# Moving three groups of work in a hybrid decoder block: where two gates are kept, how long prefetched operands rest, and which units take the seven-product steps

## The chip, the cores and the metric

The kernel runs on one core of a Trainium2 chip. The metric is the device time of one execution in microseconds (us); lower is better. Several runs of a kernel are taken and their median is compared.

## The reference, cut to what matters

The input `x` is 256 tokens by 4096 channels, float32. `w_in` is 4096 by 20480, the two matrices in `w_branch` are 2048 by 4096, `w_out` is 4096 by 4096; all are float32 and each is read once.

```python
h = rmsnorm(x, norm_w)
u_p, z_p, u_c, b_c, c_c, z_c, g_logit = split(h @ w_in)      # widths 6 x 2048, then 8192
y_pool = pool(u_p, pool_w, pool_scale) * silu(z_p)           # trailing means over 2, 4, 8, 16 tokens, a linear map per group
y_conv = b_c * conv3(c_c * u_c) * silu(z_c)                  # causal depthwise convolution of width 3
gates  = sigmoid(g_logit.reshape(256, 2, 4096) + gate_b)
merged = gates[:, 0] * (y_pool @ w_branch[0]) + gates[:, 1] * (y_conv @ w_branch[1])
out    = rmsnorm(x + merged @ w_out, final_norm_w)
```

## The kernel before, in words

**Units.** The work is a row of *units*, each giving 256 tokens by 1024 output channels. Their order: `cz0 cb0 cu0 cc0 cz1 cb1 cu1 cc1` (convolution branch: the silu gate z, then b, u, c), `pz0 pu0 pz1 pu1` (pooling branch), `g0_0 g1_0 g0_1 g1_1 g0_2 g1_2 g0_3 g1_3` (gate `g{branch}_{column}`), `b0_0 b1_0 b0_1 b1_1 ... b1_3` (the branch projections), `o0` to `o3` (the output projection). The list `units` fixes the order; everything is issued in program order on each engine.

**Steps.** A unit goes through its input channels in steps of 256; a step loads one 1 MB tile of weights into one of three buffers of `raw`. Every float32 operand is split into a rounded part ("high") and a remainder ("low"), and each product is made of three TensorE matmuls of 128x128 by 128x512. A unit's text has one letter a step. `P` is a plain step: eight products, 24 matmuls; the weights need four highs (ScalarE, `highs`) and four lows (VectorE, `lows`). `S` is a step in the Strassen-Winograd form: seven products, 21 matmuls; VectorE also makes the four sums of weight blocks in the tile `parts` (its Python name is `sums`) and splits them, and part of the results goes to the `shared` PSUM banks. `B` and `M` are the pooling steps, put into `pz1` and `g0_0` (text `HOST`). So a letter turned from P to S takes three matmuls from TensorE and gives VectorE more to do. Split weights lie in `ring`, 15 cells; `pump` prepares steps up to `AHEAD` = 4 ahead, and three past the last step of a branch unit, as far as cells and buffers are free. The first `x` units (all `c`, `p` and `g` units) have 16 steps, as have the `o` units; the branch units have 8.

**End of a unit.** The four `sums` PSUM banks are copied to the unit's destination by ScalarE (`evacuate`, into `E`, or `Y` where `dst=Y`), at the unit's end and in ScalarE's program order; the next unit's first matmuls reuse those banks. The `shared` banks go to `J` and are summed on VectorE. For a unit with `late` set, `J` is added to the destination by an accumulating DMA (`gather`, on GpSimd's queue) and the scale follows later; else VectorE adds it at once. What remains of the unit, its *epilogue* (`epi`), is a list of small tasks; one is taken from `queue` at every *tick*, that is every 6 matmuls, while the next unit multiplies.

**Gates.** A gate unit's epilogue adds the bias by DMA, waits some ticks, applies Sigmoid in `E` and stores `E` to `gates_d` in DRAM. Branch unit `b0_c` multiplies its result by gate 0, which has been brought back into `Y`, and `b1_c` multiplies by gate 1, brought back into `last_pair` (the view `spare()`). In `g1_3`'s epilogue gate `gates_d[0, 0]` is brought into `Y`. `Y` is not used by any gate unit after `g0_0`, in which the last pooling step leaves it.

**Fills.** The stationary operands sit in `arena`, whose place is shared: as the last `x` unit and later the branch units finish with their operands, those of the branch units (`y_ops`) and of `o0` (`m_ops`) are read from DRAM and split in their place. Each is a `Fill`: `fetch` moves 256 KB into a staging tile (`sa` or `sb`), and `advance` works on it at later ticks, not before `LANDING` = 8 ticks after the fetch: sums of blocks on VectorE (S operands only, four ticks then pass), then one rounding on ScalarE (`arena<-sa` in the traces), a tick later one subtraction on VectorE, after which the staging tile is free for the next fetch. `pop_fill` makes at most one advance and one fetch a tick. The fetches are issued on GpSimd's queue, in program order with the gate and bias moves.

```python
st = next((q for q in stages if not any(q is u for u in used)), None)
if st is not None:
    nxt.fetch(st)
```

**The end.** The last three steps of `o3` are taken apart by token half; after them come the last sums, the norm and the stores (`finish_half`, `finish`).

Lines in the profile: L1012 the matmuls, L57 every ScalarE activation (`act`), L60 VectorE's tensor-tensor operations (`tt`), L75 loads on SyncE's queue, L81 moves and L84 accumulating moves on GpSimd's queue.

Of the kernel before, what the change touches and what calls it, by code (L numbers as in the profile page):

```python
# [15 lines left out]
P = 128  # L16
# [15 lines left out]
TAIL = 3  # L32

SIX5 = "PPPPPSPSPSPSPSPS"
FIRST = (0, 1, 8, 2, 9, 3, 10, 11, 4, 12, 13, 5, 14, 6, 15, 7)
OPENED = 12
EIGHT3 = "PPPSPSPSSPSPSSPS"
NINE = "PSPSPSPSSPSPSSPS"
NINE_A = "PSPSSPSPSSPSPSPS"
HOST = "PPPBPPMMPSPSSPSSPSS"  # L40
TEN = "PSPSSPSSPSSPSSPS"
OUT3 = "PSPSPSPSSPSSSPPP"
B0 = "PPPPSPSP"
B1 = "PSPSPSPP"
B1_FIRST = "PPSPSPSP"
# [4 lines left out]
def hybrid_block(ctx: ExitStack, tc: tile.TileContext, x, xc, prm, rows_in, w_in, pool_w, w_branch, w_out, out):  # L50
# [32 lines left out]
    def gather(dst, src):  # L83
        return pin(nc.gpsimd.dma_start(dst, src, accum_op=ALU.add))  # L84
# [391 lines left out]
    def gap(n):  # L476
        return [None] * n
# [39 lines left out]
    def in_unit(name, col, epi, text, **kw):  # L517
        units.append(Unit(name, lambda i: w_in[col // NU, i], seq_x(text), x_ops, epi, scaled=True, **kw))
        units[-1].text = text
        return units[-1]  # L520
# [15 lines left out]
    def silu_y(late):  # L536
        def silu(t):
            act(Y[:, t], Y[:, t], AF.Silu, **(dict(scale=rin[:, t:t + 1]) if late else {}))
        return gap(18 if late else 3) + [lambda: silu(0), None, lambda: silu(1)]
# [5 lines left out]
    def conv_units(c, first):  # L545
        base = 2 * HALF + c * NU

        def b_epi(u):
            def product(t):
                stt(E[:, t], E[:, t], rin[:, t:t + 1], Y[:, t], ALU.mult, ALU.mult)  # L550
            return gap(18) + [lambda: product(0), None, lambda: product(1), None, lambda: move(g_d[c], E)]

        def c_epi(u):
            def inner(j):
                if j == 3:
                    for i in range(4):
                        act(chan(E)[:, 2 * i:2 * i + 2], bankview(i))

            def outer(j):
                act(chan(J)[:, 2 * j:2 * j + 2], bankview(j))  # L560

            def taps(j):
                v, y = chan(E)[:, 2 * j:2 * j + 2], chan(Y)
                for i in range(2):
                    b = 2 * j + i
                    kb = 8 * c + b
                    act(y[:, b], v[:, i], AF.Identity, scale=tap_col(2, kb), bias=bias_col(kb))
                for s in (1, 2):
                    for i in range(2):
                        b = 2 * j + i  # L570
                        kb = 8 * c + b
                        stt(y[:, b, s:], v[:, i, 0:T - s], tap_col(2 - s, kb), y[:, b, s:], ALU.mult, ALU.add)

            items = [lambda: move(Y, g_d[c])] + gap(6) + pairs(transposes(E, inner)) + gap(5) + pairs(transposes(Y, outer))
            for j, n in enumerate((1, 7, 8, 8)):
                items += gap(n) + [lambda j=j: taps(j)]
            return items + [None, lambda: mul(chan(E), chan(J), chan(Y)), lambda: put(y_d[1, c], chan(E))]

        u = in_unit(f"cz{c}", base + 3 * HALF, lambda u: silu_y(u.late) + (gap(4) + side_items(ND - 1) + side_items(ND - 2) if first else []),
                    FIRST if first else SIX5, dst=Y)  # L580
        u.late = not first
        in_unit(f"cb{c}", base + HALF, b_epi, TEN if c else NINE_A).late = True
        u = in_unit(f"cu{c}", base, lambda u: rescale(Y), NINE, dst=Y)
        u.late = True
        in_unit(f"cc{c}", base + 2 * HALF, c_epi, NINE_A).urgent = lambda: mul(E, E, Y)

    def pool_units(c):
        u = in_unit(f"pz{c}", HALF + c * NU, lambda u: silu_y(True) + gap(4) + band_items(c), HOST if c else SIX5, dst=Y)
        u.late = True
        in_unit(f"pu{c}", c * NU, lambda u: [], NINE).urgent = lambda: None  # L590

# [92 lines left out]
            queue.extend(gap(3) + transposes(Y, copy) + [lambda: put(y_d[0, c], chan(E))])  # L684

    def gate_unit(n, c):
        def epi(u):
            def bias(t):
                gather(E[:, t], gate_b[n, None, c * NU:(c + 1) * NU].to_broadcast([P, NU]))

            pause = gap(12)
            if (n, c) == (1, 3):
                pause = gap(5) + [lambda: move(Y, gates_d[0, 0])] + gap(6)
            items = (rescale(E) if u.late else gap(1)) + [lambda: bias(0), lambda: bias(1)] + pause + [
                lambda: act(E[:, 0], E[:, 0], AF.Sigmoid), None,
                lambda: act(E[:, 1], E[:, 1], AF.Sigmoid), lambda: move(gates_d[n, c], E)]
            return items
        text = HOST if (n, c) == (0, 0) else EIGHT3 if (n, c) == (1, 3) else TEN
        u = in_unit(f"g{n}_{c}", 6 * HALF + n * D + c * NU, epi, text)
        u.late = (n, c) != (1, 3)  # L700

    def spare():
        return last_pair["tile"].rearrange("p (a n) -> p a n", a=2)
# [1 line left out]
    def branch_unit(n, c):  # L705
        def epi(u):
            if n == 0:
                return gap(8) + [lambda: mul(Y, E, Y), None, lambda: move(spare(), gates_d[1, c])]
            turned = spare() if c < 3 else Y

            def gated():
                mul(E, E, spare())
                if c == 3:
                    last_pair["stack"].close()
                    open_last(F32R)
                    last_pair["again"] = True

            def copy(j):
                act(chan(turned)[:, 2 * j:2 * j + 2], bankview(j))

            def stored():
                put(m_d[c], chan(turned))
                merged[c] = now[0] + STORED
            return gap(2) + [gated, None, lambda: add(E, E, Y), None,
                lambda: c < 3 and move(Y, gates_d[0, c + 1])] + gap(3) + pairs(transposes(E, copy)) + [stored]

        text = (B1_LAST if c == 3 else B1 if c else B1_FIRST) if n else B0
        u = Unit(f"b{n}_{c}", lambda i: w_branch[n, c, i], seq_y(text), y_ops[n], epi)
        u.urgent, u.lead = (lambda: None), 3
        units.append(u)  # L730
# [65 lines left out]
    stages = [sa]  # L796
    fills = deque()
    now, quiet, hush = [0], [0], [0]
    LANDING, STORED, QUIET, HUSH = 8, 7, 5, 14

    def pop_fill(force=None):
        now[0] += 1
# [13 lines left out]
    conv_units(1, False)  # L816
    for c in range(2):
        pool_units(c)
    for c_ in range(4):
        for n_ in range(2):  # L820
            gate_unit(n_, c_)
    last_x = units[-1]
    for c in range(4):
        branch_unit(0, c)
# [259 lines left out]
    for u in units:  # L1084
        if u.name == "b0_0":
            last_pair["stack"].close()
            open_last(F32)
        if u is names["o1"]:
            assert not fills
            more.close()  # L1090
            open_side()

            j, items = ND - 1, list(queue)
            queue.clear()
            sides = (gap(HUSH) + [lambda: move(sa[:, 4:].rearrange("p o c -> p (o c)"),
                                                   m_d[j // 4][:, j % 4].rearrange("p k t -> p (k t)"))] + gap(8) + [
                lambda: sums_s(sa), None, None, lambda: act(side["tile"][:, 0], sa[:, 0:4]), None,
                lambda: sub(side["tile"][:, 1], sa[:, 0:4], side["tile"][:, 0].bitcast(F32))])
            items += gap(len(sides) - len(items))
            sides += gap(len(items) - len(sides))  # L1100
            queue.extend([lambda a=a, b=b: (a and a(), b and b()) for a, b in zip(items, sides)])
        if u is names["g1_0"]:
            bands_open.close()
        if u is last_x:
            side["stack"].close()
            more = ExitStack()
            ctx.enter_context(more)
            stages.append(more.enter_context(tc.tile_pool(name="more", bufs=1)).tile([P, 8, P], F32, name="sb"))
            queue_fills()
        if u is last:  # L1110
            break
        for st in u.steps:
            assert st.prepared, (u.name, st.kind)
            run_step(u, st)
            if u.text is TEN and st.kind == "S" and st.op in x_ops[:ND] and st is not u.steps[-1]:
                side_load(2 * ND - 3 - x_ops.index(st.op))
            state["now"] += 1
            if state["now"] == OPENED:
                opening.close()
                sums = ctx.enter_context(tc.tile_pool(name="parts", bufs=1)).tile([P, 4, NH], F32, name="parts")  # L1120
                open_side()
            pump()
            if u.before and st is u.steps[len(u.steps) * 3 // 4]:
                flush()
                u.before()
        flush()
        combine(u)
        queue.extend(u.epi(u))
        pump()
# [102 lines left out]
```

## Time and profile before

| what | value |
|---|---|
| median of 3 runs | 2368.66 us (2367.86 to 2369.8) |
| the profiled execution's own time | 2370.85 us |
| its span, first to last instruction | 2369.1 us |
| mean granted TensorE clock | 0.997 |
| matmuls and transposes | 10436 |
| VectorE busy | 2207.6 us (93% of the span) |
| ScalarE busy | 1538.3 us (65%) |
| moved by DMA | 570.48 MB, mean 241 GB/s |

The profiled execution's time is 1.75 us more than its span and 2.19 us above the median of the runs. An engine that is busy for nearly all the span can only give time back where it waits, so the page is read with the list of waits and with the busy time of single units. Starts in the traces are us from the first instruction; a group's idle time stands in brackets with what ended it.

### The profile page before, as it was taken

What the parts mean: (1) busy time and instruction counts of PE and PEld (TensorE: products, weight loads), DVE (VectorE), ACT (ScalarE), POOL (GpSimd) and SP (SyncE); (2) the same over time, 40 slices, a digit from 0 to 9 for tenths busy, and PEclk for the clock granted to TensorE, in tenths of its full rate; (3) what the DMA queues carried; (4) which work ended last, traced back from release to release, by engine and by line L of the source; (5) the groups of instructions that cost most, each with busy time, mean ns of one, the idle gap of its engine ahead of it and who ended that gap; (6) DMA issues with size and microseconds to landing.
All of it is one profiled execution on the core that took longest, in us unless ns stands there. A gap on an engine that the chain in (4) does not pass through costs nothing. (4 is left out here: it accounts for less than half of the span.)

```text
span 2369.1 us, 28319 instructions
## 1 busy us (share of the span) xinstructions
PE 2345.7 (99%) x10436; PEld 1941.2 (82%) x10436; DVE 2207.6 (93%) x2433; ACT 1538.3 (65%) x1829; POOL 132.2 (6%) x193
## 2 busy tenths in 40 slices
PE   9999999999999999999999999999999999999997
PEld 7888888888888888888888888888878888888886
DVE  8899989999979979979999999999988898899998
ACT  6666656666666656656677767776655656566665
POOL 0000000000001000000000000001100001000000
PEclk9999999999999999999999999999999999999999
DMA  9667755775756656646877788778866757667886
GB/s 348 234 234 241 227 198 213 243 242 218 233 211 215 229 175 226 227 177 228 269 249 262 244 270 257 254 252 275 286 225 237 265 208 253 244 212 262 269 260 258
DMA packets 94330, 570.48 MB, mean 241 GB/s; under 512 B 10288, under 2 KB 10544, under 8 KB 33264
## 3 DMA queue, kind: packets, MB, share of 16 engines
q1 hardware_dynamic: 69824, 485.39, 56.8%
q0 software_dynamic: 23792, 82.06, 13.3%
q8 instruction: 81, 1.33, 0.2%
q10 hardware_dynamic: 576, 1.24, 0.1%
q14 instruction: 57, 0.47, 0.1%
HBM read 523.56 MB, written 27.26 MB: 233 GB/s over the span
## 5 line engine op out<-in xcount | busy, mean ns | idle before, releaser
L1012 PE MATMUL sums<-ring,arena 128*128 128x512 f32 x7071 | 1655.2, 390 | 9.2 <-ACT E L57 6.5
L1012 PEld LDWEIGHTS sums<-ring,arena 128*128 128x128 f32 x7071 | 1326.9, 188 | 286.2 <-ACT E L57 7.9
L60 DVE TENSOR_TENSOR ring<-raw,ring 128x1024 fp32r<-128x1024 f32 (+2 forms) x889 | 965.2, 1105 | 96.3 <-ACT ring L57 95.5
L57 ACT ACTIVATE ring<-raw 128x1024 fp32r<-128x1024 f32 (+3 forms) x682 | 790.7, 1196 | 229.4 <-PE sums L1012 111.4
L57 ACT ACTIVATE ring<-parts 128x512 fp32r<-128x512 f32 (+1 forms) x670 | 500.2, 761 | 484.7 <-DVE parts L60 425.3
L1012 PE MATMUL shared<-ring,arena 128*128 128x512 f32 x2193 | 529.5, 389 | 0.0
L60 DVE TENSOR_TENSOR ring<-parts,ring 128x1024 fp32r<-128x1024 f32 (+1 forms) x464 | 515.2, 1152 | 4.6 <-ACT ring L57 4.5
L1012 PEld LDWEIGHTS shared<-ring,arena 128*128 128x128 f32 x2193 | 411.7, 188 | 85.4
L60 DVE TENSOR_TENSOR parts<-parts,raw 128x512 f32<-128x512 f32 x436 | 297.7, 683 | 0.0
L60 DVE TENSOR_TENSOR parts<-raw 128x1024 f32<-128x1024 f32 x218 | 265.2, 1217 | 12.2 <-DMA raw<-in_w_in_dram 5.5
L60 DVE TENSOR_TENSOR J<-J 128x512 f32<-128x512 f32 (+1 forms) x90 | 78.1, 868 | 9.2 <-ACT J L57 6.3
L1012 PE MATMUL sums<-ring,last_pair 128*128 128x512 f32 x306 | 76.3, 389 | 0.6 <-DVE ring L60 0.6
L57 ACT ACTIVATE J<-shared 128x512 f32<-128x512 f32 x128 | 69.2, 604 | 2.3 <-PE shared L1012 0.5
L1012 PEld LDWEIGHTS sums<-ring,last_pair 128*128 128x128 f32 x306 | 57.4, 188 | 12.9 <-DVE ring L60 1.1
L84 POOL DMA_DIRECT2D E<-J x24 | 29.2, 1456 | 463.3 <-DVE J L60 324.9
L1012 PE MATMUL shared<-ring,last_pair 128*128 128x512 f32 x216 | 52.2, 390 | 0.0
L1012 PE MATMUL shared<-ring,side 128*128 128x512 f32 x207 | 50.7, 389 | 0.0
L57 ACT ACTIVATE E<-sums 128x512 f32<-128x512 f32 x80 | 44.8, 594 | 4.8 <-PE sums L1012 2.3
L1012 PEld LDWEIGHTS shared<-ring,last_pair 128*128 128x128 f32 x216 | 40.5, 188 | 8.8 <-DVE ring L60 0.4
L1012 PEld LDWEIGHTS shared<-ring,side 128*128 128x128 f32 x207 | 38.9, 188 | 8.1
L57 ACT ACTIVATE E<-E 128x1024 f32<-128x1024 f32 x20 | 20.9, 1046 | 4.6 <-DMA E<-in_x_dram 4.6
L84 POOL DMA_DIRECT2D Y<-J x10 | 12.2, 1453 | 199.2 <-issue 126.4
(132 smaller groups left out, 637.2 us busy)
## 6 DMA issues: line engine op xcount, KB each, us to landing
raw<-in_w_in_dram SPq DMA_DIRECT2D x318, 1024.0 KB, 4.9
raw<-in_w_branch_dram SPq DMA_DIRECT2D x64, 1024.0 KB, 4.8
raw<-in_w_out_dram SPq DMA_DIRECT2D x64, 1024.0 KB, 4.9
E<-J POOLq DMA_DIRECT2D x24, 512.0 KB, 8.3
E<-in_rows_dram POOLq DMA_DIRECT2D x16, 512.0 KB, 8.9
gates_d<-E POOLq DMA_DIRECT2D x8, 1024.0 KB, 6.5
Y<-J POOLq DMA_DIRECT2D x10, 512.0 KB, 9.5
y_d<-E POOLq DMA_DIRECT2D x8, 512.0 KB, 7.8
```

The costliest lines, as they stand in the source:

```text
L57: return pin(nc.scalar.activation(dst, src, func, **kw))
L60: return pin(nc.vector.tensor_tensor(out=dst, in0=a, in1=b, op=op))
L84: return pin(nc.gpsimd.dma_start(dst, src, accum_op=ALU.add))
L1012: pin(nc.tensor.matmul(ps, lhs, rhs, start=n == 0, stop=n == u.total[b] - 1))
```

## The change

- **Gates.** The order of the gate units becomes `g0_0 g0_1 g1_1 g0_2 g1_2 g0_3 g1_3 g1_0`. `g0_0` has `Y` as its destination and its gate stays there; `g1_0`, now the last `x` unit and the one that isn't late, writes its Sigmoid from `E` into `spare()`. These two gates are neither stored nor brought back; the pause in the epilogue of the last gate unit has no move of `Y` any more.
- **Fills.** `LANDING` is 12 ticks and not 8, and there is a third staging tile, `sc`.
- **Texts.** `cz1` and `pz0` have seven S steps and not six (`SIX5` to `SEVEN5`; `o0` keeps `SIX5`), the last gate unit has seven and not eight (`EIGHT3` to `SEVEN3`), `o3` has seven and not eight (`OUT3`).

```diff
+SEVEN5 = "PPPPPSPSSPSPSSPS"
-EIGHT3 = "PPPSPSPSSPSPSSPS"
+SEVEN3 = "PPPSPSPSPSPSPSPS"
-OUT3 = "PSPSPSPSSPSSSPPP"
+OUT3 = "PSPSPSPSPSPSSPPP"
...
-                    FIRST if first else SIX5, dst=Y)
+                    FIRST if first else SEVEN5, dst=Y)
...
-        u = in_unit(f"pz{c}", ..., HOST if c else SIX5, dst=Y)
+        u = in_unit(f"pz{c}", ..., HOST if c else SEVEN5, dst=Y)
...
     def gate_unit(n, c):
+        first, final = (n, c) == (0, 0), (n, c) == (1, 0)
+
         def epi(u):
+            d = u.dst
+
             def bias(t):
-                gather(E[:, t], gate_b[n, None, c * NU:(c + 1) * NU].to_broadcast([P, NU]))
-
-            pause = gap(12)
-            if (n, c) == (1, 3):
-                pause = gap(5) + [lambda: move(Y, gates_d[0, 0])] + gap(6)
-            items = (rescale(E) if u.late else gap(1)) + [lambda: bias(0), lambda: bias(1)] + pause + [
-                lambda: act(E[:, 0], E[:, 0], AF.Sigmoid), None,
-                lambda: act(E[:, 1], E[:, 1], AF.Sigmoid), lambda: move(gates_d[n, c], E)]
-            return items
-        text = HOST if (n, c) == (0, 0) else EIGHT3 if (n, c) == (1, 3) else TEN
-        u = in_unit(f"g{n}_{c}", 6 * HALF + n * D + c * NU, epi, text)
-        u.late = (n, c) != (1, 3)
+                gather(d[:, t], gate_b[n, None, c * NU:(c + 1) * NU].to_broadcast([P, NU]))
+
+            def gate(t):
+                act((spare() if final else d)[:, t], d[:, t], AF.Sigmoid)
+
+            items = (rescale(d) if u.late else gap(1)) + [lambda: bias(0), lambda: bias(1)] + gap(12) + [
+                lambda: gate(0), None, lambda: gate(1)]
+            return items if first or final else items + [lambda: move(gates_d[n, c], E)]
+        text = HOST if first else SEVEN3 if final else TEN
+        u = in_unit(f"g{n}_{c}", 6 * HALF + n * D + c * NU, epi, text, dst=Y if first else E)
+        u.late = not final
...
-                return gap(8) + [lambda: mul(Y, E, Y), None, lambda: move(spare(), gates_d[1, c])]
+                return gap(8) + [lambda: mul(Y, E, Y), None, lambda: c and move(spare(), gates_d[1, c])]
...
-    LANDING, STORED, QUIET, HUSH = 8, 7, 5, 14
+    LANDING, STORED, QUIET, HUSH = 12, 7, 5, 14
...
-    for c_ in range(4):
-        for n_ in range(2):
-            gate_unit(n_, c_)
+    gate_unit(0, 0)
+    for c in range(1, 4):
+        for n in range(2):
+            gate_unit(n, c)
+    gate_unit(1, 0)
...
-        if u is names["g1_0"]:
+        if u is names["g0_1"]:
             bands_open.close()
...
-            stages.append(more.enter_context(tc.tile_pool(name="more", bufs=1)).tile([P, 8, P], F32, name="sb"))
+            pool = more.enter_context(tc.tile_pool(name="more", bufs=1))
+            stages.extend(pool.tile([P, 8, P], F32, name=name) for name in ("sb", "sc"))
```

More of the change, by code (lines that the diff above doesn't have):

```diff
@@ L587, in pool_units @@
     def pool_units(c):
-        u = in_unit(f"pz{c}", HALF + c * NU, lambda u: silu_y(True) + gap(4) + band_items(c), HOST if c else SIX5, dst=Y)
+        u = in_unit(f"pz{c}", HALF + c * NU, lambda u: silu_y(True) + gap(4) + band_items(c), HOST if c else SEVEN5, dst=Y)
         u.late = True
```

## The prediction

> **What bounds the kernel now.** I read the page first, then TensorE's waits, then the chain of waits for the pace of undisturbed matmuls, then busy time by unit.
>
> ```profile
> PE 2345.7 (99%) x10436; PEld 1941.2 (82%) x10436; DVE 2207.6 (93%) x2433; ACT 1538.3 (65%) x1829; POOL 132.2 (6%) x193
> L1012 PE MATMUL sums<-ring,arena 128*128 128x512 f32 x7071 | 1655.2, 390 | 9.2 <-ACT E L57 6.5
> PE sums L1012 <- ACT E L57: 6.5, 2, 5.5
> PE sums L1012 <- DVE ring L60: 2.5, 2, 1.8
> 2060.28 7.48 PE sums L1012 x33
> 2057.56 2.72 PE shared L1012 x12
> ...
> 338.14:424.74 86.60, 86.60 (x399) 72.03 (x398) 79.31 (x89) 54.28 (x69) 2.10 (x3) 1.00 0.59 219
> 424.74:504.98 80.24, 80.24 (x355) 66.46 (x354) 80.00 (x89) 54.73 (x65) 3.06 (x3) 1.00 0.70 229
> 666.82:753.42 86.60, 86.60 (x399) 72.03 (x398) 79.37 (x90) 54.80 (x70) 2.09 (x3) 1.00 0.62 219
> 1594.24:1675.84 81.60, 81.60 (x362) 67.59 (x361) 78.12 (x92) 57.64 (x68) 10.23 (x15) 1.00 0.81 262
> 1675.84:1723.70 47.86, 42.32 (x188) 34.74 (x186) 42.37 (x48) 30.82 (x38) 5.05 (x8) 0.99 0.90 310
> 1723.70:1767.82 44.12, 44.12 (x183) 36.34 (x184) 39.28 (x41) 27.71 (x32) 1.61 (x3) 0.94 0.62 213
> 2273.64:2356.80 83.16, 82.53 (x361) 67.16 (x359) 79.45 (x91) 49.04 (x61) 6.54 (x8) 1.00 0.77 261
> ```
>
> TensorE is the bound: an undisturbed matmul takes 7.48/33 = 0.2267 us, and nearly the whole span is such a stream. A tick, six matmuls, is 1.36 us. The unit rows are, in order, cz1, cb1, pz0, g1_3, b0_0, b1_0 and o3; after the length stand the busy times of PE, PEld, DVE, ACT, POOL, then granted clock, DMA share and GB/s. Only around b0_0 is much lost: 5.5 us idle at its end, and a granted clock of 0.94 in the unit behind it. Nothing is to be won elsewhere except a microsecond here and there. The question is whether the change removes that wait, and whether it makes another.
>
> **What the wait at b0_0's end is made of.** The timeline there:
>
> ```profile
> 1717.96 0.63 ACT L57 ACTIVATE arena<-sa 128x512 fp32r<-128x512 f32 x1 [3.87 <-DMA sa<-y_d]
> 1720.75 1.58 ACT L57 ACTIVATE ring<-raw 128x512 fp32r<-128x512 f32 x2 [2.15 <-DMA raw<-in_w_branch_dram]
> 1722.23 0.93 ACT L57 ACTIVATE arena<-sb 128x896 fp32r<-128x896 f32 x1
> 1723.07 2.04 ACT L57 ACTIVATE E<-sums 128x512 f32<-128x512 f32 x4
> 1723.70 8.47 PE L1012 MATMUL sums<-ring,arena 128*128 128x512 f32 x25 [5.54 <-ACT E L57]
> ...
> DMA packets 1274, 7.81 MB, mean 339 GB/s; under 512 B 178, under 2 KB 178, under 8 KB 464
> raw<-in_w_branch_dram SPq DMA_DIRECT2D x5, 1024.0 KB, 9.1
> Y<-gates_d POOLq DMA_DIRECT2D x1, 1024.0 KB, 10.1
> gates_d<-E POOLq DMA_DIRECT2D x1, 1024.0 KB, 7.8
> ...
> DMA packets 3899, 23.93 MB, mean 255 GB/s; under 512 B 405, under 2 KB 405, under 8 KB 1301
> raw<-in_w_in_dram SPq DMA_DIRECT2D x19, 1024.0 KB, 5.5
> ```
>
> TensorE stopped at 1723.70 - 5.54 = 1718.16 and waited for ScalarE to empty the `sums` banks. ScalarE works in order, and ahead of the copy to `E` stood a fill whose data had not landed (3.87 us), then the highs of a step whose weights had not landed (2.15 us), then another fill. The four DMA rows below are those of 1694 to 1717 us, the last two those of 1500 to 1594 us, most of it g0_3. In the first stretch a weight load takes 9.1 us from issue to landing, in the second 5.5 us, and there TensorE has no wait. Of the 7.81 MB of the first stretch, 2 MB are gate 0,0 coming back and gate 1,3 going out.
>
> **Gates.** Both transfers leave this place: gate 0,0 stays in `Y`, and the last gate unit, now g1_0, stores nothing. The rate needed falls to (7.81 - 2)/23 us = 253 GB/s, that of g0_3, so I take g0_3's 5.5 us for a weight load. The load waited for at 1720.75 then lands about 9.1 - 5.5 = 3.6 us earlier, at 1717.1, before TensorE is done at 1718.16. The store that g1_3 made at this place it makes in g1_0, beside a unit with no wait now. Sigmoid is written to another tile at the same ticks. Gate 1,0's return behind b0_0 goes too; nothing waited for it, so I count nothing. Holding `Y` through the gate units costs nothing since none of them writes it.
>
> **Fills.** Four ticks more before the rounding are 4 x 1.36 = 5.4 us, more than the 3.87 us waited here. The second such place is the end of b1_3:
>
> ```profile
> 2016.78 0.54 POOL L81 DMA_DIRECT2D sb<-m_d  x1 [3.47 <-issue]
> 2023.07 0.63 ACT L57 ACTIVATE arena<-sb 128x512 fp32r<-128x512 f32 x1 [4.58 <-DMA sb<-m_d]
> 2026.88 3.47 PE L1012 MATMUL sums<-ring,arena 128*128 128x512 f32 x14 [1.00 <-ACT E L57]
> ...
> 2098.38 1.08 DVE L60 TENSOR_TENSOR arena<-sb,arena 128x896 fp32r<-128x896 f32 x1
> 2107.03 2.20 PE L1012 MATMUL sums<-ring,arena 128*128 128x512 f32 x9
> ```
>
> A fill issued at 2016.78 held ScalarE for 4.58 us, and TensorE idled 1.00 us; 5.4 us more cover that. So both waits go, 5.54 + 1.00 us. Behind the first one 25 matmuls took 8.47 us; at 0.2267 us from start to start, and 0.39 us for the last as in the page's row, they need 5.83: another 2.6 us. At the second place the clock did not fall visibly.
> The Trainium skill ("TensorE: Matmul & The Clock Gate", Part 1) says that an idle window of about 3.4 us halves TensorE's clock until about as long of busy time has passed. The 0.94 behind the 5.54 us idle agrees; worked out from the page, 3.4 us at half rate lose some 1.7 us, an estimate, and the sum would be 0.9 us less good by it.
> The longer pause costs throughput: a staging tile holds a plain fill 13 ticks, not 9. Three tiles make up for it, 3/13 against 2/9 fills a tick. Late is only the last fill of o0. Its source is stored last; before, with two tiles, the last four are fetched at ticks T, T+1, T+13 and T+15 and the last is done at T+28. After, three are fetched at once, the fourth gets a tile at T+17 and is done at T+34; set against the matmuls of o0 this comes to some 39 matmuls or 8.8 us later. Above, its subtraction ended at 2099.46 and TensorE began the step that uses it at 2107.03: 7.57 us to spare. That leaves -1.3 us, of which the first two matmuls, which don't read the remainder, give 0.45 back. I take a new wait of 0.7 us; its bounds are 0 (VectorE less far behind) and 2.
>
> **Texts.** Two P become S and two S become P: 3 matmuls each way, 0.68 us, nothing in sum. VectorE's price of a letter, from cb1:
>
> ```profile
> 431.84 1.22 DVE L60 TENSOR_TENSOR parts<-raw 128x1024 f32<-128x1024 f32 x1
> 438.26 1.21 DVE L60 TENSOR_TENSOR parts<-raw 128x1024 f32<-128x1024 f32 x1
> 444.61 2.35 DVE L60 TENSOR_TENSOR ring<-raw,ring 128x1024 fp32r<-128x1024 f32 x2
> ...
> PE sums L1012 <- DVE ring L60: 0.6, 1, 0.6
> 2336.45 3.18 PE L1012 MATMUL shared<-ring,last_pair 128*128 128x512 f32 x12
> 2340.15 16.68 PE L1012 MATMUL sums<-ring,arena 128*128 128x512 f32 x72
> 2356.58 0.68 DVE L60 TENSOR_TENSOR E<-sums,E 128x512 f32<-128x512 f32 x1
> 2357.91 0.68 DVE L60 TENSOR_TENSOR E<-sums,E 128x512 f32<-128x512 f32 x1
> ```
>
> Two S steps start 6.42 us apart, a P step takes 2.35: 4.1 us a letter. cz1 and pz0 go from 79.3 to 83.4 us of VectorE in 85.9 us; cb1, with four pairs of neighbouring S and 80.00 of 80.24, shows no TensorE wait. I take 0; what it costs if that slack is no cover stands below. g1_0 takes 4.1 us off VectorE just ahead of b0_0, which there is busy for 42.37 us where TensorE worked 42.32; this helps the loads of b0_0 further, uncounted. In o3 three S in four steps ended in a wait of 0.6 us, and the 12 matmuls at 2336.45 took 3.18 where 2.72 is usual: 1.1 us, gone with 4.1 us less on VectorE. Also, the last two additions of the results started at 2356.58 and 2357.91, though TensorE ended at 2340.15 + 16.68 = 2356.83: VectorE, late since o3, still had the first half's norm to finish. With 4.1 us less it is in time, and the last starts about 1.0 us sooner.
>
> **Sum.** -5.5 - 2.6 - 1.0 - 1.1 - 1.0 + 0.7 = -10.5 us. The profiled execution's 2370.85 becomes 2360.3; the median of the runs is 2.19 lower, and 2368.66 becomes 2358.1. A measurement can tell about 0.2%, 4.7 us, from no change.
>
> **Rivals.**
> *Weights still late.* Loads keep their 9.1 us, since the same loads and fills still meet, now three fills at once. For it: five loads in 23 us lie close together by themselves. Against it: the needed rate falls to g0_3's. Then the 2.15 us wait still ends at 1720.75, the highs at 1722.33, and 4.2 us idle and 2.6 us slow matmuls stay: 2358.1 + 6.8 = 2364.9. The Trainium skill ("DMA: Bandwidth & Descriptors", Queues, rings and completion order) has every DMA engine take turns between the queues, so that more open fills would slow each load; by that rule this is the outcome, and the 9.1 against 5.5 us bears it out in part.
> *The last fill of o0.* If VectorE is late there by several us more, idle time grows past 5 us and the clock falls again: 5.5 + 2.6 instead of 0.7, 2365.5. For it: the spare time is negative by my own count. Against: it takes some 5 us more than the 1.3 us counted, and the list of waits has only two on VectorE's writes to `ring` in the whole run.
> *VectorE in the z units (slower).* If none of the 7.29 us that VectorE stands idle in cz1 can be used, the unit grows to 79.31 + 4.1 + 7.29 = 90.7 us, 4.8 more than 85.9, and the two cost 9.5 us. Split on their four pairs of S, that is 2.4 us each; if the clock falls after each, 2.6 x 4 comes on top: 19.9, and 2358.1 + 19.9 = 2378.0. It decides from 15.3 us on, where the result is 4.7 us slower than now. cb1 speaks against it.
> *It doesn't act.* Were the waits at b0_0 caused elsewhere, only the other terms would be left, -1.0 - 1.1 - 1.0 + 0.7 = -2.4: 2366.3.
>
> **Chances and range.** Forecast 0.79, weights late 0.10, last fill 0.05, z units 0.04, no action 0.02. All gains without the new wait, and 1.5 us of spread between runs, give 2355.9; upward the range takes in the rival of 2364.9. Faster by over 0.2%: the forecast and the better part of the second and third case, 0.86; within 0.2%: 0.10; slower: 0.04.
>
> **What would show it.** Right: no wait of TensorE on `E` over 1 us, a granted clock of 1.00 in b1_0, b0_0 in about 42.5 us, weight loads there near 5.5 us, no ScalarE wait on `DMA sa<-` of 3 us, the last addition within 0.3 us of TensorE's end. Wrong: TensorE waits in cz1 to cc1 or in o0, or an unchanged 5 us behind b0_0.

## The result and the profile after

| kernel | median of runs, us | lowest to highest | profiled execution, us | span, us |
|---|---|---|---|---|
| before, beside after | 2367.88 (8 runs) | 2366.16 to 2369.8 | 2370.85 | 2369.1 |
| after | 2362.69 (8 runs) | 2361.56 to 2363.43 | 2362.26 | 2360.3 |

The ratio after to before is 0.9978, 95% interval 0.9967 to 0.9988: 5.2 us faster, where 10.5 were forecast. The two profiled executions differ by 8.59 us.

The change was run again later (after_again, below) and was then 6.0 us faster.

The page's busy times, its row of the costliest group, and three rows of the list of TensorE's waits (us in total, times, longest), after:

```profile
PE 2344.8 (99%) x10436; PEld 1939.8 (82%) x10436; DVE 2206.1 (93%) x2430; ACT 1535.1 (65%) x1832; POOL 131.3 (6%) x189
L1018 PE MATMUL sums<-ring,arena 128*128 128x512 f32 x7041 | 1648.4, 390 | 2.5 <-ACT E L58 0.9 <-DVE ring L766 0.8 <-DVE ring L61 0.7
PE sums L1018 <- ACT E L58: 0.9, 2, 0.6
PE shared L458 <- DVE E L61: 0.8, 1, 0.8
PE sums L1018 <- DVE ring L61: 0.7, 2, 0.4
```

Idle time ahead of the main matmuls fell from 9.2 to 2.5 us, and the wait on `E` from 6.5 to 0.9. New is a wait on the transposes' `shared` for VectorE, 0.8 us. The unit rows, in order cz1, pz0, g1_0 (the last gate unit now), b0_0, b1_0, b0_1 and o3, with the columns of the prediction:

```profile
337.87:424.52 86.65, 86.24 (x396) 71.29 (x395) 80.05 (x90) 53.42 (x68) 2.10 (x3) 1.00 0.57 207
666.69:753.18 86.49, 86.24 (x397) 71.37 (x395) 79.83 (x89) 53.59 (x67) 2.09 (x3) 1.00 0.56 207
1594.18:1676.46 82.28, 82.28 (x364) 68.13 (x363) 74.94 (x87) 55.70 (x66) 10.24 (x15) 1.00 0.83 275
1676.46:1718.81 42.35, 42.32 (x187) 34.72 (x185) 38.88 (x46) 30.65 (x39) 4.94 (x8) 1.00 0.78 258
1718.81:1761.21 42.40, 41.80 (x183) 34.27 (x183) 41.82 (x44) 26.51 (x33) 0.10 (x1) 1.00 0.56 209
1761.21:1806.40 45.19, 44.35 (x202) 36.60 (x203) 38.17 (x36) 26.18 (x33) 4.18 (x7) 1.00 0.77 280
2266.88:2349.32 82.44, 82.44 (x364) 67.94 (x362) 77.24 (x87) 48.78 (x62) 6.58 (x8) 1.00 0.80 276
```

b0_0 fell from 47.86 to 42.35 us. b1_0 fell from 44.12 to 42.40, its clock from 0.94 to 1.00. o3 has three matmuls more (0.68 us) and yet is shorter, 83.16 to 82.44; the last gate unit has three more too and is longer by 82.28 - 81.60 = 0.68 us, so it has no wait. cz1 and pz0 have three matmuls fewer and didn't become shorter by 0.68: 86.60 to 86.65 and 86.49. b1_0 and b0_1 still are above what their matmuls need (below). ScalarE's timeline at b0_0's end and the transfers of 1694 to 1717 us, after:

```profile
1716.26 0.64 ACT L58 ACTIVATE arena<-sb 128x512 fp32r<-128x512 f32 x1
1716.78 1.50 ACT L58 ACTIVATE ring<-raw 128x1536 fp32r<-128x1536 f32 x1
1718.16 2.06 ACT L58 ACTIVATE E<-sums 128x512 f32<-128x512 f32 x4
...
DMA packets 1050, 6.46 MB, mean 281 GB/s; under 512 B 144, under 2 KB 144, under 8 KB 380
raw<-in_w_branch_dram SPq DMA_DIRECT2D x6, 1024.0 KB, 5.2
```

ScalarE passes from the fill to the highs of the weights to the copy out of `sums` with no wait; before, it waited 3.87 and 2.15 us in these places. A weight load takes 5.2 us where it took 9.1, in the median of each stretch. In o0 and at the very end:

```profile
2098.17 1.08 DVE L61 TENSOR_TENSOR arena<-sa,arena 128x896 fp32r<-128x896 f32 x1
2100.28 2.20 PE L1018 MATMUL sums<-ring,arena 128*128 128x512 f32 x9
...
2347.80 1.52 PE L1018 MATMUL sums<-ring,last_pair 128*128 128x512 f32 x6
2349.36 0.69 DVE L61 TENSOR_TENSOR E<-sums,E 128x512 f32<-128x512 f32 x1 [0.55 <-PE sums L1018]
```

From 2009.81 on, across the end of b1_3, TensorE runs without a gap:

```profile
2009.81 14.46 PE L1018 MATMUL sums<-ring,arena 128*128 128x512 f32 x63
```

Its 63 matmuls need 62 x 0.2267 + 0.39 = 14.45 us. The last fill of o0 was done at 2098.17 + 1.08 = 2099.25, 1.03 us ahead of its step. The last addition starts 0.04 us after TensorE's end at 2349.32; before, it was 1.08.

### The profile page after: what moved, and what is told of

The parts are those of the page before. It is cut to its first block, busy times and chain, and to the rows that moved or that the text cites. A ratio compares the mean times of both kernels' runs of the same rounds, so it can differ in the third digit from the quotient of the medians.

```text
span 2360.3 us, 28303 instructions
## 1 busy us (share of the span) xinstructions
PE 2344.8 (99%) x10436; PEld 1939.8 (82%) x10436; DVE 2206.1 (93%) x2430; ACT 1535.1 (65%) x1832; POOL 131.3 (6%) x189
## 4 chain that ended last, share of the span: by engine, by line
PE 93%; DVE 4%; DMA 1%; issue 1%; ACT 1%; SPq 0%; DVEq 0%; ACTq 0%
PE sums L1018 67%; PE shared L1018 24%; DVE ring L61 2%; DVE parts L61 1%; PE shared L672 1%; DMA raw<-in_w_in_dram 1%; PE shared L458 1%; DVE E L61 1%; ACT ring L58 0%; DVE Y L73 0%; DVE J L61 0%; PE shared L648 0%; ACT J L58 0%; DVE E L73 0%; ACT E L58 0%
## 5 line engine op out<-in xcount | busy, mean ns | idle before, releaser
L61 DVE TENSOR_TENSOR ring<-raw,ring 128x1024 fp32r<-128x1024 f32 (+3 forms) x884 | 964.4, 1110 | 92.9 <-ACT ring L58 91.5
L1018 PE MATMUL shared<-ring,arena 128*128 128x512 f32 x2217 | 535.4, 389 | 0.0
L1018 PE MATMUL sums<-ring,last_pair 128*128 128x512 f32 x336 | 83.0, 389 | 0.0
L1018 PEld LDWEIGHTS sums<-ring,last_pair 128*128 128x128 f32 x336 | 63.0, 188 | 13.2 <-DVE ring L61 0.2
L1018 PE MATMUL shared<-ring,last_pair 128*128 128x512 f32 x192 | 46.1, 389 | 0.0
L672 PE MATMUL shared<-ring 128*128 128x512 f32 x96 | 22.1, 389 | 0.0
```

Source lines behind the costliest of these rows:

```text
L61: return pin(nc.vector.tensor_tensor(out=dst, in0=a, in1=b, op=op))
L672: pin(nc.tensor.matmul(o, a, b, start=(k, i) == (0, 0), stop=(k, i) == (3, 2)))
L1018: pin(nc.tensor.matmul(ps, lhs, rhs, start=n == 0, stop=n == u.total[b] - 1))
```

## The experiments

Eleven kernels were run, one of them twice, in three batches (p1 to p4; after_again to p7_better; p7_again to p10), each batch beside runs of the kernel before on the same chip (their medians: 2368.86, 2368.3, 2369.15). First the change was taken apart, then the fills alone, then a version that gives VectorE the time it lacks.

| run | median, us | ratio to before, 95% interval |
|---|---|---|
| p1_gates: gates part alone | 2365.26 | 0.9986 (0.9978 to 0.9995) |
| p2_fills: pause of 12 and third tile alone | 2362.1 | 0.9976 (0.9966 to 0.9986) |
| p3_texts: step texts alone | 2368.51 | 1.0001 (0.9992 to 1.001) |
| p4_gates_fills: both, old texts | 2362.01 | 0.9969 (0.9958 to 0.998) |
| after_again | 2362.31 | 0.9977 (0.9967 to 0.9987) |
| p5_pause: pause of 12, two tiles | 2409.28 | 1.0173 (1.0159 to 1.0187) |
| p6_third: third tile, pause of 8 | 2370.07 | 1.0009 (1.0 to 1.0018) |
| p7_better: after, S steps placed otherwise | 2360.48 | 0.9968 (0.9955 to 0.998) |
| p7_again: the same | 2360.53 | 0.9964 (0.995 to 0.9977) |
| p8_no_gates: p7 without the gates part | 2366.51 | 0.9988 (0.998 to 0.9997) |
| p9_relief: p4, one S less in b1_0 | 2362.02 | 0.9969 (0.9958 to 0.9981) |
| p10_ten: p7 with a pause of 10 | 2359.2 | 0.996 (0.9947 to 0.9972) |

### Gates alone

```diff
 # after, with the fills and texts of before
-    LANDING, STORED, QUIET, HUSH = 12, 7, 5, 14
+    LANDING, STORED, QUIET, HUSH = 8, 7, 5, 14
-            stages.extend(... for name in ("sb", "sc"))
+            stages.extend(... for name in ("sb",))
```

> The gates part alone on the kernel before (gate 0,0 kept in Y, gate 1,0 made last and written in place, order of the gate units changed; two staging tiles, pause of 8 ticks, all texts as before). Theory 'crowding' (the wait at the end of b0_0 comes from weight loads slowed by the two gate transfers): in the profile the wait at b0_0's end falls from 5.5 us to under 1 us, the slow matmuls behind it go, weight loads there take about 5.5 us and not 9.1, the 1.0 us at b1_3's end stays; the median falls by 4 to 8 us against before. Theory 'pause' (it comes from ScalarE waiting for a fill that has not landed): at least 3 us of the wait at b0_0 stay, the median falls by under 2.5 us.

3.6 us faster than before by the medians. Timeline, load and unit rows (b0_0, b1_0) of p1_gates:

```profile
1717.88 1.58 ACT L58 ACTIVATE ring<-raw 128x512 fp32r<-128x512 f32 x2 [2.86 <-DMA raw<-in_w_branch_dram]
raw<-in_w_branch_dram SPq DMA_DIRECT2D x4, 1024.0 KB, 6.2
1676.24:1720.84 44.60, 42.33 (x188) 34.74 (x186) 40.95 (x46) 30.85 (x38) 4.12 (x7) 1.00 0.82 279
1720.84:1764.05 43.21, 43.21 (x183) 35.61 (x184) 40.39 (x44) 27.90 (x32) 1.07 (x2) 0.96 0.55 199
```

Loads fall from 9.1 to 6.2 us, as the theory of the crowding has it, and yet ScalarE waits 2.86 us for one and TensorE 44.60 - 42.33 = 2.3 us. Taking 2 MB out of the way isn't enough. In b1_0 TensorE doesn't wait; its 43.21 us are those of a lower clock.

### Fills alone

```diff
 # before, with
-    LANDING, STORED, QUIET, HUSH = 8, 7, 5, 14
+    LANDING, STORED, QUIET, HUSH = 12, 7, 5, 14
-            stages.append(... name="sb"))
+            stages.extend(... for name in ("sb", "sc"))
```

> The fills part alone on the kernel before (third staging tile, pause of 12 ticks). Theory 'crowding': weight loads in b0_0 still take about 9 us, the wait at b0_0's end stays at 3 to 5.5 us, only the 1.0 us at b1_3's end goes: median 1 to 2.5 us less than before. Theory 'pause': both waits go and with them the slow matmuls, median 4 to 8 us less. Both theories: the last fill of o0 is ready 1 to 2 us before its step, with no wait of TensorE.

6.8 us faster. Timeline, load and unit rows (b0_0, b1_0) of p2_fills:

```profile
1718.22 1.58 ACT L57 ACTIVATE ring<-raw 128x512 fp32r<-128x512 f32 x2 [2.90 <-DMA raw<-in_w_branch_dram]
raw<-in_w_branch_dram SPq DMA_DIRECT2D x5, 1024.0 KB, 6.5
1675.88:1720.85 44.97, 42.64 (x187) 34.66 (x185) 41.65 (x47) 31.45 (x39) 5.64 (x10) 1.00 0.94 327
1720.85:1762.46 41.61, 41.61 (x183) 34.47 (x184) 39.92 (x43) 27.82 (x32) 0.99 (x2) 1.00 0.63 223
```

The same 2.3 us are left, so gates and fills each remove a good half of the wait, and neither theory of a single cause holds. The wait at b1_3's end is gone here as in after. What p2_fills has over p1_gates is that and the clock in b1_0: its 41.61 us is the bare time of that unit's 183 matmuls, the measure for after's 42.40. The theory of the crowding had loads of 9 us here, as before; with 8.60 MB at 374 GB/s in the stretch, more than before, they took 6.5. The amount moved alone doesn't set the time of a load.

### Texts alone, and gates with fills

```diff
 # p3: before, with
-EIGHT3 = "PPPSPSPSSPSPSSPS"
+EIGHT3 = "PPPSPSPSPSPSPSPS"
-OUT3 = "PSPSPSPSSPSSSPPP"
+OUT3 = "PSPSPSPSPSPSSPPP"
-                    FIRST if first else SIX5, dst=Y)     # and in pz
+                    FIRST if first else SEVEN5, dst=Y)
 # p4: after, with the reverse of these
```

> The texts alone on the kernel before (seven S in cz1 and pz0, seven and not eight in g1_3 and o3). Both theories: waits of 0.5 to 0.8 us at the ends of cz1 and pz0 (together 1.2 to 1.5 us), the 1.1 us in o3 and about 1 us behind the last matmul gone, so -0.5 to -1.5 us from these. If VectorE's lateness at the start of b0_0 had a share in the wait there (4.1 us less of its work in g1_3), that wait falls too, by up to 4 us; 'crowding' and 'pause' both have it stay above 3 us.

> The changed kernel with the texts of before (six S in cz1 and pz0, eight in the last gate unit and in o3). No waits in cz1 and pz0, the 1.1 us in o3 and the 1 us at the end are back. If the parts add up, it lies 0.5 to 1.5 us above the changed kernel (median of that: 5.2 us under before), so 3.5 to 5 us under before; if the texts' relief of VectorE in the last gate unit is needed for b0_0, a wait of 1 us or more comes back there and it lies 2 us or more above the changed kernel.

p3 moved nothing: the wait on `E` at b0_0 is still there.

```profile
PE sums L1013 <- ACT E L58: 6.6, 3, 4.9
```

p4 isn't above after either, 2362.01 against 2362.69 and 2362.31. So the texts, as they stand in the change, bring nothing that the runs can tell; in after's profile they save 2.4 us in o3 and at the end and lose 1.3 in the z units. p4's rows of b1_0 and b0_1, with the waits of TensorE there:

```profile
1718.43:1761.09 42.66, 41.80 (x185) 34.10 (x183) 41.18 (x43) 25.99 (x30) 0.54 (x1) 1.00 0.57 203
1761.09:1806.63 45.54, 44.36 (x203) 36.62 (x203) 37.73 (x37) 25.54 (x34) 4.17 (x7) 1.00 0.75 271
PE shared L458 <- DVE E L61: 1.2, 1, 1.2
PE sums L1018 <- ACT E L58: 0.9, 1, 0.9
```

These two waits are in after as well (0.8 and 0.6 us) and came with the removal of the wait at b0_0, whatever the texts. They also hide the gates part: p4 and p2_fills, in the same batch, differ by 0.1 us (2362.01 and 2362.1), though b0_0 takes 42.49 us in p4 and 44.97 in p2. Of those 2.5 us b1_0 (42.66 against 41.61) and b0_1 (45.54 against some 44.3) take 2.3 back. On top of the fills and with the old texts, the gates part is worth nothing that the runs can tell.

### Pause alone and third tile alone

```diff
 # p5: before, with
-    LANDING, STORED, QUIET, HUSH = 8, 7, 5, 14
+    LANDING, STORED, QUIET, HUSH = 12, 7, 5, 14
 # p6: before, with
-            stages.append(... name="sb"))
+            stages.extend(... for name in ("sb", "sc"))
```

> The changed kernel once more, beside the runs of this batch, so that they can be compared with it: about 5 to 7 us under before, waits of TensorE of 0.5 to 0.8 us at the ends of cz1 and pz0 and about 2 us in b1_0 and b0_1.

> On the kernel before only the pause of 12 ticks, with two staging tiles. Theory 'pause' (what helped in the fills part is that ScalarE no longer waits for a landing): both waits on the copies to E go, median 4 to 7 us under before. Theory 'third tile' (what helped is that three tiles let the fills be done sooner; the pause by itself makes them late): counted by ticks, the fills of the last three steps of b1_0 and of o0's last step are then done only when their step asks for them, and with VectorE 4 to 9 us behind the program order each such step waits 4 to 10 us: 10 to 30 us slower than before.

> On the kernel before only the third staging tile, pause of 8 ticks. Theory 'third tile': counted by ticks the last fill of b1_0 is done 114 matmuls sooner than with the longer pause, the roundings lie 78 or more matmuls ahead of the copies to E at b0_0's end, so ScalarE's waits for landings are hidden: the wait at b0_0's end falls to 0 to 2.5 us, median 5 to 8 us under before. Theory 'pause': ScalarE still waits 3 to 5 us for landings just ahead of the copies to E, median within 2.5 us of before.

after_again repeats after. p5 is 41 us slower; 10 to 30 were expected of a pause that makes the fills late. Its waits, and the row of b1_0:

```profile
PE sums L1012 <- ACT arena L57: 20.4, 5, 6.3
PE sums L1012 <- DVE arena L60: 7.0, 2, 3.7
1718.42:1795.05 76.63, 54.45 (x185) 41.15 (x184) 48.28 (x55) 30.79 (x35) 2.69 (x5) 0.78 0.44 150
```

TensorE waits for its stationary operands in `arena` themselves, 27 us in all: with two tiles each held longer, the fills come too late for the steps that use them; b1_0 grows by 32 us, and the clock in it is 0.78. p6 is 1.8 us slower than before. The theory that the third tile carries the gain of the fills expected it 5 to 8 us under before, and falls. Timeline and waits of p6 around b0_0:

```profile
ACT arena L57 <- DMA sc<-y_d: 8.2, 2, 4.3
1723.16 1.58 ACT L57 ACTIVATE ring<-raw 128x512 fp32r<-128x512 f32 x2 [3.42 <-DMA raw<-in_w_branch_dram]
1724.64 2.04 ACT L57 ACTIVATE E<-sums 128x512 f32<-128x512 f32 x4
PE sums L1012 <- ACT E L57: 4.4, 3, 3.9
```

With the short pause ScalarE stands 8.2 us before fills of the new tile that haven't landed. The copy to `E` doesn't stand right behind these: right ahead of it is a wait of 3.42 us for weights, whose load was issued only at 1716.97 (1711.11 in before). That the load was late because ScalarE was late in freeing its buffer is likely, not shown. So a long pause needs the tile and the tile needs the long pause; only together do they save 6.8 us.

### VectorE's time

```diff
 # after, with
-SEVEN5 = "PPPPPSPSSPSPSSPS"
+SEVEN5 = "PPPPPSSPSSPSPSPS"
-B1_FIRST = "PPSPSPSP"
+B1_FIRST = "PPSPPSPP"
```

> The changed kernel with two texts altered: in cz1 and pz0 the same seven S with the neighbouring pairs early (PPPPPSSPSSPSPSPS), and b1_0 with two S and not three (PPSPPSPP; 3 matmuls more, 0.68 us, 4.1 us less on VectorE). If VectorE's lateness makes the waits at the ends of cz1 and pz0 (0.69 and 0.54 us) and in b1_0 and b0_1 (0.76 and 1.18 us), all four fall under 0.3 us and the median lies 1.5 to 2.5 us under the changed kernel. If the waits have another cause (landings, ScalarE), they stay and it lies 0 to 1 us above.

> The changed kernel with both altered texts (early pairs of S in cz1 and pz0, two S in b1_0) once more, for the comparison with the runs of this batch: 7 to 8 us under before, no wait of TensorE over 0.5 us behind cz0.

The theory here was that what is left in after is VectorE being late: in cz1 and pz0 because the S steps stand too close to the end, in b1_0 and b0_1 because VectorE no longer has the 5.5 us in which TensorE stood still at b0_0. The edit keeps the number of S in the z units and puts three of them one step earlier; b1_0 gets one S less, three matmuls more. Rows of cz1, pz0, b1_0 and b0_1 of p7_again:

```profile
338.23:424.15 85.92, 85.92 (x397) 71.44 (x396) 81.20 (x92) 54.37 (x70) 2.10 (x3) 1.00 0.59 211
666.23:752.14 85.91, 85.91 (x396) 71.44 (x395) 81.23 (x91) 54.84 (x71) 2.10 (x3) 1.00 0.58 211
1717.76:1760.05 42.29, 42.29 (x186) 35.02 (x187) 39.79 (x38) 25.92 (x29) 0.00 (x0) 1.00 0.59 214
1760.05:1804.03 43.98, 43.98 (x204) 36.57 (x202) 34.75 (x35) 24.97 (x33) 4.18 (x7) 1.00 0.75 270
```

No wait is left in any of the four. Against after, cz1 is 0.73, pz0 0.58 and b0_1 1.21 us shorter with the same matmuls, and b1_0 0.11 with 0.68 us more of them: 2.6 us in all, of which the medians show 1.8. For the z units and for these two the profiles show the cause: the same work with VectorE earlier or less loaded has no wait.

```diff
 # p8: before, with the fills, the texts and the two edits of p7
 # p9: p4 with the B1_FIRST of p7
 # p10: p7, with
-    LANDING, STORED, QUIET, HUSH = 12, 7, 5, 14
+    LANDING, STORED, QUIET, HUSH = 10, 7, 5, 14
```

> All of p7_again but the gates part (order of the gate units, stores and returns of the gates as before). Theory 'displaced' (with the fills part in, the gates part does take 2.5 us off b0_0, and it showed no gain only because VectorE, without that pause, was late by the same 2 us in b1_0 and b0_1): with VectorE relieved in b1_0 the wait of 2 to 2.5 us at b0_0's end stands alone, weight loads there take 7 to 8 us, and it lies 1.5 to 2.5 us above p7_again. Rival 'no use' (with the fills part in, the two transfers cost nothing in ordinary executions): within 0.5 us of p7_again.

> p4_gates_fills (gates and fills parts, texts of before) with two S and not three in b1_0. Theory 'VectorE': the waits of 1.0 and 1.4 us in b1_0 and b0_1 fall under 0.4 us, for 0.68 us of matmuls: about 1.5 us under p4_gates_fills. Against p7_again it tells what the changed texts are worth once their waits in cz1 and pz0 are gone: p7_again 0.5 to 1.5 us lower by o3 and the end, or no difference if the waits there are those of single executions.

> p7_again with a pause of 10 ticks and not 12 (13.6 us). If landings in b0_0 take 5 to 6 us behind 3 to 8 us of VectorE's lateness, 10 ticks suffice nearly everywhere: within 0.5 us of p7_again, and ScalarE's waits for staging tiles stay under 1 us each. If 12 ticks are needed: waits of 1 to 3 us for landings come back on ScalarE and it lies 0.5 to 3 us above.

p8 is 6.0 us above p7_again, where 1.5 to 2.5 were expected: with everything else in place the gates part is worth more than alone (3.6) and more than on top of the fills with the old texts (0.1). Transfers at b0_0 and the wait there in p8:

```profile
DMA packets 1369, 8.54 MB, mean 371 GB/s; under 512 B 184, under 2 KB 184, under 8 KB 472
raw<-in_w_branch_dram SPq DMA_DIRECT2D x5, 1024.0 KB, 9.6
last_pair<-gates_d POOLq DMA_DIRECT2D x1, 1024.0 KB, 12.9
PE sums L1013 <- ACT E L58: 4.8, 1, 4.8
```

Loads of 9.6 us and a wait of 4.8 are back. It isn't the amount: p2_fills moved as much (8.60 MB) with loads of 6.5 us and a wait of 2.3. What differs in the order of the moves is, above all, gate 1,0's return into `last_pair`. GpSimd issues it at 1711.61 in p8, behind the load issued at 1710.21 that ScalarE then waits for, and only after that wait in p2_fills (1721.31) and in before (1727.88). The prediction counted nothing for this transfer. That it makes the difference is likely; no run has it alone. p9 has no wait in b1_0 and b0_1 either, but its median is that of p4 (2362.02 and 2362.01, in different batches), not 1.5 us lower: a miss, and so the gain of one S less in b1_0 is shown in profiles only. p7_again, in the same batch as p9, is 1.5 us under it; so with the S steps well placed the texts do pay. p10 is the fastest, 1.3 us under p7_again, which neither expectation had; in b0_0 ScalarE waits 2.8 us for a fill, and TensorE not at all. It isn't shown that the shorter pause does that: p7_again issues its last store at 2351.71 and p10 at 2351.48, and their spans are 2358.6 and 2357.4, so 1.0 of the 1.2 us between the spans lies behind the last store's issue. What sets that stretch stays open.

## Why the prediction was right, and its gain twice the measured one

The forecast direction and the mechanism held; the rows of after answer the sum term by term, profile against profile:

- **Wait at b0_0**, -5.5 us: 47.86 to 42.35, -5.5. Weight loads were taken at 5.5 us and measured 5.2. The sharing out was off: the working laid the fill's 3.87 us to the pause and the weights' 2.15 us to the gates; in p1 and p2 the wait for the fill is gone with either part, and the wait for weights is 2.86 and 2.90 us with either, and goes only with both. A step was missing, too: the working was content with a landing at 1717.1, ahead of TensorE's end. But ScalarE's highs, a fill and the first copies lay between landing and TensorE's start, 1723.70 - 1720.75 = 2.95 us, so by its own numbers 1.9 us of wait would have been left. p1, with a landing at 1717.88, has such a wait of 2.3 us. That the whole 5.5 went is owed to a load faster than assumed and to the pause, by which no fill stands there. The load waited for (issued at 1711.11 in before, 1711.83 in p1, 1710.33 in p2, 1711.13 in after), from the views of the transfers of that microsecond, in this order, with the us to landing at the end of each line:

```profile
raw<-in_w_branch_dram SPq DMA_DIRECT2D x1, 1024.0 KB, 9.6
raw<-in_w_branch_dram SPq DMA_DIRECT2D x1, 1024.0 KB, 6.0
raw<-in_w_branch_dram SPq DMA_DIRECT2D x1, 1024.0 KB, 7.9
raw<-in_w_branch_dram SPq DMA_DIRECT2D x1, 1024.0 KB, 4.7
```

- **Slow matmuls behind it**, -2.6: b1_0 was 44.12 and is 41.61 without a wait (p2), -2.5.
- **b1_3's end**, -1.0: the 1.00 us wait is gone. **o3**, -1.1: 83.16 to 82.44 with 0.68 us of matmuls more, -1.4. **Last addition**, -1.0: 1.08 to 0.04 us behind TensorE.
- **Last fill of o0**, +0.7: nothing. The count gave -1.3 us to spare; measured were 1.03. The subtraction came 6.5 us nearer to its step (7.57 to 1.03), not 8.8; the lower bound that was named came true. Why the shift is smaller stays open.
- **z units**, 0: +0.73 and +0.58. The step that failed is the 0 taken from cb1. cz1 has its seven S in its last eleven steps, cb1 ten in sixteen: about as dense, but VectorE's idle time in cz1 lies under the five P steps ahead of them and isn't there to be used: after, it is busy for 20.77 of the unit's first 27.23 us and for 59.29 of the 59.42 behind them. p7 shows that their places count: with the same seven S, three of them one step earlier, the waits are gone. Waits in cz1 were among the prediction's signs of being wrong; one came, of 0.4 us; the rest of the 0.73 us is longer busy time of TensorE (86.24 us against 85.92 in p7_again). The rival of the z units thus acted, at 1.3 us of the 9.5 it was priced at, and without the clock falling.
- **Not in the sum:** b1_0 +0.8 (42.40 against 41.61) and b0_1 +0.9. The wait at b0_0 had hidden that VectorE had no time to spare behind it, as p7 and p9, with no wait there, bear out: the prediction asked what is late next only in o0. b0_1 of before, which took 0.86 us less than after's 45.19:

```profile
1767.82:1812.15 44.33, 44.21 (x204) 36.50 (x202) 36.53 (x36) 24.97 (x33) 3.66 (x6) 1.00 0.72 266
```

The lengths as they stand, matmuls added and removed included (b0_0 -5.5, b1_0 -1.7, b0_1 +0.9, b1_3 -1.2, o3 -0.7, last gate unit +0.7, last addition -1.0, the rest below 0.5 each) add up to -8.5 us, of the -8.8 between the two spans. So of 10.5 forecast 8.6 came in the profiles, and 5.2 in the medians. The second loss is the step "the median of the runs is 2.19 lower, and 2368.66 becomes 2358.1": it took the same offset for after as for before. But the profiled execution of before lay 2370.85 - 2367.88 = 2.97 us above its median, that of after 0.43 below: 3.4 us of difference. The terms were sized in a long execution. That it is the wait at b0_0 that differs from execution to execution is argued, not shown: before's 27 runs of the first batch spread from 2365.32 to 2374.02, p4's from 2360.39 to 2363.19. The others point the same way, if not without exception: the runs of kernels with a wait of over 2 us there (p1, p2, p3, p6, p8) spread over 4.0 to 6.3 us, those of after, p4, p7, p9 and p10 over 0.6 to 3.0, after_again's over 4.9.

The rivals: *weights still late* did not act in after, where loads took 5.2 us with three fills open; with either part alone it did (2.86 and 2.90 us). The rule of the Trainium skill ("DMA: Bandwidth & Descriptors", Queues, rings and completion order), that engines take turns between queues, did not give that outcome in after. p8's 9.6 us at 371 GB/s would fit it, but p2_fills's 6.5 at 374, with three fills as well, doesn't bear out that more open fills mean slower loads. *It doesn't act* is out.

## What to carry to other kernels

When a wait goes, ask of every engine that used it to catch up how much time it has left in the next two units; here 1.7 of the 8.0 us won at b0_0 came back so, and in the profiles one S step less there, at 0.68 us of matmuls, got it back. A prefetch's pause and the number of its buffers are one setting: apart they cost 41 us and 2 us, together they saved 7. And set the size of a wait by several executions: one profile's offset from its median isn't the offset of the kernel without that wait.

## What was not expected of the hardware

- The clock behind a short idle time differs: after the 2.3 us at b0_0's end it was 0.96 in b1_0 in p1_gates and 1.00 in p2_fills. In p1 it was 0.50 from 1722 to 1724 us, and this cost 43.21 - 41.61 = 1.6 us; in p2 it was 1.00 throughout. It was 0.94 behind 5.54 us (before; 0.50 from 1724 to 1728), at a cost of 2.5 us, and 0.78 in p5's b1_0, with 22 us of idle time in it. The Trainium skill ("TensorE: Matmul & The Clock Gate", Part 1) gives an idle window of about 3.4 us; in p1 the clock fell after less, 2.27 us.
- A 1 MB weight load took 5.2 us at a mean of 281 GB/s (after), 5.5 at 255 and 9.1 at 339 (before), 6.2 at 276 (p1), 9.6 at 371 (p8), but 6.5 at 374 (p2): loads above 9 us came only in stretches above 300 GB/s, yet the mean rate alone doesn't tell them.
